# RG-LRU and gates in buffers of their own beside the RWKV, its products in halves of two PSUM banks, and the input projection in five passes

## The chip, the cores and the metric

The kernel runs on one core of one Trainium2 chip. The metric is device time in microseconds of one execution; the time before is the median of three. One further execution was profiled, and its trace gives every duration below. Engines: PE (matrix products), DVE (vector), ACT (scalar), POOL (GpSimd) and SP, whose queue issues the transfers here.

## The reference, cut to what matters

One block of a hybrid encoder, 2048 tokens behind 16 meta tokens, width 1024, float32. Three head groups read the same normed input through one projection; their outputs go through one output projection, then a feed-forward part (FFN) with a convolution.

```python
p = rms_norm(h, norm_mix_pre[l]) @ w_in[l]
pa = p[..., :A_COLS]                     # 512 columns: RG-LRU, xa and ya
pb = p[..., A_COLS:A_COLS + B_COLS]      # q, k, v of 512 columns, 8 forget gates
pc = p[..., A_COLS + B_COLS:]            # 1024 columns: RWKV-7
oa = rg_lru_group(xa, ya, ...)           # conv of 4, two gates, h = a * h + b over time, times gelu(ya)
ob = forgetting_attention_group(...)     # causal softmax(q k + c_i - c_j) v, c = cumsum(log sigmoid(gate))
oc, v_own = rwkv7_group(pc, ...)         # S = S diag(w) - (S kk)(kk a)^T + v k^T over time, o = S r
mixed = jnp.concatenate([oa, ob, oc], axis=-1) @ w_out[l]
h = h + rms_norm(mixed, norm_mix_post[l])
f = causal_dwconv(rms_norm(h, norm_ffn_pre[l]) @ ffn_up[l], ffn_conv[l])
gate, val = jnp.split(f, 2, axis=-1)
f = (jax.nn.gelu(gate, approximate=True) * val) @ ffn_down[l]
h = h + rms_norm(f, norm_ffn_post[l])
```

RG-LRU and RWKV run over time, so their token blocks come one after the other; attention needs the keys and values of all earlier tokens and the sums of the gates.

## The kernel before, in words

The program is written with a tile framework: pools give named tiles with a number of buffers (`bufs`), and a scheduler orders each engine's instructions, by and large as the code is written. Each engine and SP's queue works through its row in order.

- **Input projection.** The tokens come in three parts of 7, 6 and 4 token tiles (784, 768 and 512 tokens), each in two blocks. For a part, `w_in_norm` loads x, norms it on DVE and ACT (L96, `xt` at L108) and transposes it on PE (tile `pst`, L121), with a split into a high and a low half (`xh` L127, `xl` L128). `w_in_part` then goes through units: the gates (tile `psf`), 8 units "c" (RWKV), 4 "a" (RG-LRU), 4 each of k, v and q. Each loads its weights (L143, 512 KB, tile `raw`) and makes three products for one (`mm3`, L150 to L152, tile `psp`). ACT and DVE take the results out of PSUM (`stp`, `sth`, `stl`, `stv`), and SP stores them in DRAM (`scr_p`, `scr_qh`, `scr_kl` and so on).
- **Recurrences.** `Beside(PACE)` advances a generator 1.5 steps for each unit of the projection. `recurrences` runs, for a part, the gates' sums (`gate_block`, L345 to L389), and for three blocks of tokens each `lru_block` (L1228 to L1281), the RWKV block (`R.block`, products in the tiles `eps` and `rps`) and the ending of the block before, one after the other. LRU and gates borrow RWKV's tiles k, r, sq, e and raw. All short products (`eps`) share one PSUM bank, tag "ae", one product at a time. PSUM stands at 5 banks for the projection (`ps_mm`), 1 for "ae", 2 for `rps`.
- **Sums of FFN weights.** `weight_sums` makes sums of blocks of the FFN's weights on POOL (L1436) in one buffer: 22 steps `us` (load L1441, store L1450) and 10 steps `ds` (load L1454, store L1463), each of 2 MB.
- **Attention.** It starts behind the last unit: half 0 is the first half of the queries (from the first K load), in which 8 heads load K, V and Q, PE makes maxima (`mx`) and scores (`sc`), ACT the exponentials (`p`, L558), POOL the masks and sums (`acc`, L588), PE the products with v (`po`), DVE the maxima (`mc`, L492, L495) and the output (`o`). What is left of the recurrences lies in half 0.
- Then follow the other half, the output projection and the FFN.

Of the kernel before, what the change touches and what calls it, by code (L numbers as in the profile page):

```python
# [257 lines left out]
def w_in_part(core, pools, psum, w_in, blocks, scr):  # L258
    yield from w_in_gate(core, pools, psum, w_in, blocks, scr)
    units = [("c", 2056 + P * i) for i in range(8)] + [("a", P * i) for i in range(4)]  # L260
    units += [(s, c + P * i) for s, c in (("k", 1024), ("v", 1536), ("q", 512)) for i in range(4)]
# [77 lines left out]
def gate_block(core, R, f_bias, scr, tl):  # L339
# [10 lines left out]
    x = new("k")  # L350
    nc.sync.dma_start(x, scr["f"][:, t0 : t0 + n])
    a = new("r")
# [7 lines left out]
    call = R.t([NH, 512], "sq")[:, : o + n]  # L360
# [7 lines left out]
    ch, cl = new("k", F32R), new("r", F32R)  # L368
# [304 lines left out]
def columns(core, pool, psum, vecs, name, out=None):  # L673
# [9 lines left out]
    while todo:  # L683
# [6 lines left out]
        if at == P or not todo:  # L690
            ps = psum.tile([P, 512], F32, tag="ae", bufs=1, name=core.n("pscol"))
# [21 lines left out]
def rwkv_consts(core, pool, psum, w):  # L713
# [34 lines left out]
    ps = psum.tile([P, 512], F32, tag="ae", bufs=1, name=core.n("psspr"))  # L748
# [31 lines left out]
    rst = c.tile([P, 8 * CH], F32, name="rst")  # L780
# [6 lines left out]


    u1 = c.tile([P, 256], F32, name="unit1")
    nc.vector.memset(u1[:], 0.0)  # L790
    nc.vector.memset(u1[:, 0:256:17], 1.0)
    u2 = c.tile([P, 128], F32, name="unit2")
    nc.vector.memset(u2[:], 0.0)
    nc.vector.memset(u2[0:64, 0:128:17], 1.0)
    nc.vector.memset(u2[64:128, 8:128:17], 1.0)
    k["unit"] = {1: u1, 2: u2}
# [3 lines left out]
class Rwkv:  # L800
# [23 lines left out]
    def pe(self):  # L824

        return self.epsum.tile([P, 512], F32, tag="ae", name=self.core.n("eps"), bufs=1)

    def raw(self, row, c0, c1):

        raw = self.t([P, 2, 260], "raw", bufs=2)[:, :, : c1 - c0]  # L830
# [13 lines left out]
    def block(self, b):  # L844
# [22 lines left out]
        for p in range(2):  # L867
            cs_ = slice(P * p, P * p + P)
            ps = self.pe()
            nc.tensor.matmul(ps[:, :n], k["up"][0:64, cs_], flat(wa[:])[0:64], start=True, stop=True)  # L870
            nc.scalar.activation(flat(half(sig, p)), ps[:, :n], AF.Tanh, scale=0.5, bias=pcol("w0_h", p))
        nc.gpsimd.tensor_scalar(sig, sig, 0.5, 0.5, op0=ALU.mult, op1=ALU.add)
        for p in range(2):
            cs_ = slice(P * p, P * p + P)
            ps = self.pe()
            nc.tensor.matmul(ps[:, :n], k["up"][64:128, cs_], flat(wa[:])[64:128], start=True, stop=True)
            nc.scalar.activation(flat(half(av, p)), ps[:, :n], AF.Tanh, scale=0.5, bias=pcol("a0_h", p))
# [5 lines left out]
        for p in range(2):  # L883
            nc.tensor.matmul(ps[:4, :n], k["gat"][:, p], flat(half(sq, p)), start=p == 0, stop=p == 1)
        ks2, kinv, ktmp = (self.t([P, 256], s)[:4, :n] for s in ("ia", "ix", "itmp"))
# [3 lines left out]
        nc.vector.tensor_tensor_scan(  # L889
            flat(cs), k["rst"][:, : 2 * n], flat(sig), 0.0, op0=ALU.mult, op1=ALU.add  # L890
        )
# [9 lines left out]
        for p in range(2):  # L901
            ps = self.pe()
            nc.tensor.matmul(ps[:, :n], k["spr"][:, p], kinv, start=True, stop=True)
            stt(flat(half(kt, p)), flat(half(kt, p)), pcol("k_k", p), ps[:, :n], op0=ALU.mult, op1=ALU.mult)
# [15 lines left out]
        for p in range(2):  # L920
            stt(half(kp, p), half(kp, p), pcol("r_k", p), half(r, p), op0=ALU.mult, op1=ALU.mult)
            ps = self.pe()
            nc.tensor.matmul(ps[:, :n], k["bones"][:], flat(half(kp, p)), start=True, stop=True)
            tt(half(bon, p), ps[:, :n].rearrange("p (c t) -> p c t", t=CH), half(rav, p)[:, :, 2], op=ALU.mult)
# [3 lines left out]
    def chunks(self, b, nch, sg, rav, bk, wc, bon):  # L928
# [55 lines left out]
        nc.vector.tensor_copy(ix[:np_, : 16 * jw], k["unit"][parts][:np_, :])  # L984
# [237 lines left out]
def lru_block(core, R, scr, k, b):  # L1222
# [7 lines left out]
    def tl(s):  # L1230
        return R.t([P, 2, 256], s)[:, :, :n]

    raw = R.raw(0, c0 - 3, c0 + n)
    u, r, g = tl("k"), tl("r"), tl("sq")
    e = R.t([P, 2, 2, 256], "e")
    al, y = e[:, 0, :, :n], e[:, 1, :, :n]
    for p in range(2):
# [9 lines left out]
        ps = R.pe()  # L1247
        nc.tensor.matmul(ps[:, :n], k["ga_w"][:, p], up, start=True, stop=True)
        nc.scalar.activation(r[:, p], ps[:, :n], AF.Abs, bias=k["ga_b"][:, pc])
        nc.vector.tensor_scalar(al[:, p], ps[:, :n], k["ga_b"][:, pc], 0.0, op0=ALU.add, op1=ALU.min)  # L1250
        ps = R.pe()
        nc.tensor.matmul(ps[:, :n], k["gx_w"][:, p], up, start=True, stop=True)
        nc.scalar.activation(g[:, p], ps[:, :n], AF.Tanh, scale=0.5, bias=k["rate"][:, 2, pc])
# [4 lines left out]
    yield  # L1258
    for p in range(2):
        pc = slice(p, p + 1)  # L1260
        nc.scalar.activation(al[:, p], r[:, p], AF.Exp, scale=k["rate"][:, 0, pc])
        nc.scalar.activation(r[:, p], r[:, p], AF.Tanh, scale=k["rate"][:, 1, pc])

# [4 lines left out]
    stt(g, g, 0.5, r, op0=ALU.mult, op1=ALU.mult)  # L1268
    for p in range(2):
# [4 lines left out]
    ya = R.raw(256, c0, c0 + n)  # L1274
# [721 lines left out]
```

## Time and profile before

| | us |
|---|---|
| median of 3 runs | 3178.94 (3169.02 to 3179.52) |
| profiled execution, its own time | 3171.78 |
| span of its trace | 3170.1 |
| projection, last product psp | to about 905 |
| K loads of attention's half 0 | from 908 |
| last instruction of the recurrences | about 1231 |
| end of attention's half 0 | about 1240 |
| first product of the output projection | 1290 |
| FFN up | from about 1704 to 2700 |

A window's row gives its bounds and length, the busy time of the engines with the number of instructions, then the granted clock of PE, the DMA share, and GB/s. A row of a wait gives engine, tile and line, what it waited for, the total, the number of waits and the longest. A row of a group ends with minimum, median and maximum in ns, and the first and last start in us. A matmul of plain float32 mostly stands as two records in the trace and as one in the order of instructions.

### The profile page before, as it was taken

The page shows a single profiled execution, that of the slowest core. Times are in us where ns is not written, and L with a number is a line of the kernel's source. Part 1 is how long each engine was busy: PE and PEld are TensorE (multiplying, and loading weights), DVE is VectorE, ACT ScalarE, POOL GpSimd, SP SyncE. Part 2 cuts the span into 40 slices and gives each one's busy share as a digit, 9 for nine tenths or more (in the row PEclk, how much of TensorE's full clock was granted, in tenths as well). Part 3 has the DMA queues.
Part 4 walks back from the last instruction along what each step waited for, and adds up shares of the span by engine and source line. Part 5 has one row for each costly group of instructions (what it writes and reads, how often), then busy time and mean ns, then how long its engine had stood idle before and what let it go on. Part 6 is the DMA issues. An engine that isn't in the chain of part 4 may idle for free. (4 is left out here: it accounts for less than half of the span.)

```text
span 3170.1 us, 53032 instructions
## 1 busy us (share of the span) xinstructions
PE 2974.7 (94%) x18509; PEld 2476.6 (78%) x18509; DVE 2194.2 (69%) x4603; ACT 1444.0 (46%) x2723; POOL 1267.2 (40%) x1439
## 2 busy tenths in 40 slices
PE   6988899999989998999999799999999999999998
PEld 6977788888865554455447699999999999787776
DVE  6247665776677767677756777787778787557777
ACT  4134334344534434444443466666666665424322
POOL 3333343201023344444651234433543334556655
PEclk9989899999987778999999999999999999999999
DMA  6777766543342226444426365555555565535444
GB/s 198 232 225 241 212 196 225 189 132 104 98 124 67 71 64 154 108 109 106 99 59 207 119 181 177 166 170 167 165 167 164 169 187 160 184 103 170 140 160 140
DMA packets 494412, 484.12 MB, mean 153 GB/s; under 512 B 83680, under 2 KB 408618, under 8 KB 488496
## 3 DMA queue, kind: packets, MB, share of 16 engines
q1 hardware_dynamic: 493248, 480.26, 50.8%
q8 instruction: 146, 2.39, 0.3%
q14 instruction: 122, 1.00, 0.1%
q0 software_dynamic: 384, 0.39, 0.0%
q10 hardware_dynamic: 512, 0.07, 0.0%
HBM read 354.66 MB, written 125.87 MB: 152 GB/s over the span
## 5 line engine op out<-in xcount | busy, mean ns | idle before, releaser
L150 PE MATMUL psu<-xo,uw 128*128 128x344 f32 x1848 | 587.8, 323 | 8.2 <-DVE wx L1346 4.8
L151 PE MATMUL psu<-xo,uw 128*128 128x344 f32 x1848 | 593.0, 321 | 1.0 <-DVE xo L1418 1.0
L152 PE MATMUL psu<-xo,uw 128*128 128x344 f32 x1848 | 582.6, 320 | 0.0
L152 PE MATMUL psp<-xh,wl 128*128 128x384 f32 (+2 forms) x1152 | 380.3, 330 | 1.1 <-DVE wl L145 1.0
L150 PE MATMUL psp<-xh,wh 128*128 128x384 f32 (+2 forms) x1152 | 381.2, 331 | 0.0
L151 PE MATMUL psp<-xl,wh 128*128 128x384 f32 (+2 forms) x1152 | 378.2, 328 | 0.0
L150 PEld LDWEIGHTS psu<-xo,uw 128*128 128x128 f32 x1848 | 347.0, 189 | 9.7 <-DVE wx L1346 5.2
L151 PEld LDWEIGHTS psu<-xo,uw 128*128 128x128 f32 x1848 | 348.4, 189 | 1.3 <-DVE xo L1418 1.3
L152 PEld LDWEIGHTS psu<-xo,uw 128*128 128x128 f32 x1848 | 346.8, 189 | 0.0
L1417 ACT ACTIVATE uw<-uq 128x512 fp32r<-128x512 f32 x462 | 286.9, 626 | 98.3 <-PE psu L152 47.8
L1418 DVE TENSOR_TENSOR uw<-uq,uw 128x512 fp32r<-128x512 f32 x330 | 285.5, 869 | 63.6 <-ACT uw L1417 59.2
L558 ACT ACTIVATE p<-sc,bias 128x512 f32<-128x512 f32 (+2 forms) x360 | 203.3, 586 | 254.5 <-PE sc L556 215.9
L588 POOL TENSOR_TENSOR acc<-acc,p 128x512 f32<-128x512 f32 (+3 forms) x208 | 226.9, 1091 | 181.8 <-ACT p L558 152.6
L1418 POOL TENSOR_TENSOR uw<-uq,uw 128x512 fp32r<-128x512 f32 x132 | 180.9, 1370 | 266.6 <-ACT uw L1417 232.5
L1517 DVE SCALAR_TENSOR_TENSOR uy<-psu,ffn_cols,uy 128x342 f32<-128x342 f32 (+1 forms) x396 | 224.0, 568 | 88.2 <-ACT uy L1515 87.1
L1523 POOL TENSOR_TENSOR uy<-uy,uy 128x342 f32<-128x342 f32 (+1 forms) x132 | 136.7, 1036 | 326.1 <-DVE uy L1517 136.5
L492 DVE TENSOR_REDUCE mc<-mx 128x1 f32<-128x400 f32 (+5 forms) x320 | 173.2, 556 | 111.4 <-PE mx L489 110.0
L152 PEld LDWEIGHTS psp<-xh,wl 128*128 128x128 f32 x1152 | 220.0, 191 | 8.2 <-issue 3.7
L151 PEld LDWEIGHTS psp<-xl,wh 128*128 128x128 f32 x1152 | 219.8, 191 | 7.8 <-issue 6.4
L150 PEld LDWEIGHTS psp<-xh,wh 128*128 128x128 f32 x1152 | 220.0, 191 | 6.0 <-issue 3.8
L1436 POOL TENSOR_TENSOR us<-us 128x512 f32<-128x512 f32 x88 | 128.3, 1458 | 221.0 <-DMA us<-in_ffn_up_dram 197.3
L567 PE MATMUL po<-p,v 128*64 128x512 f32 (+3 forms) x720 | 186.3, 555 | 8.4 <-ACT p L558 2.9
(415 smaller groups left out, 6442.1 us busy)
## 6 DMA issues: line engine op xcount, KB each, us to landing
uq<-scr_us SPq DMA_DIRECT2D x264, 256.0 KB
uq<-in_ffn_up_dram SPq DMA_DIRECT2D x198, 256.0 KB
raw<-in_w_in_dram SPq DMA_DIRECT2D x72, 512.0 KB
us<-in_ffn_up_dram SPq DMA_DIRECT2D x44, 512.0 KB
scr_us<-us SPq DMA_DIRECT2D x22, 1024.0 KB
u<-scr_ff SPq DMA_DIRECT2D x88, 256.0 KB
scr_ff<-uy SPq DMA_DIRECT2D x110, 171.0 KB
q<-scr_qh SPq DMA_DIRECT2D x96, 128.0 KB
```

The costliest lines, as they stand in the source:

```text
L150: nc.tensor.matmul(out, ah, bh, start=first, stop=False, skip_group_check=more)
L151: nc.tensor.matmul(out, ah, bl, start=False, stop=False, skip_group_check=more)
L152: nc.tensor.matmul(out, al, bh, start=False, stop=last, skip_group_check=more)
L492: self.reduced = nc.vector.tensor_reduce(mc[:rows, i, ci : ci + 1], ps[:rows, :full], axis=AX.X, op=ALU.max)
L558: last = nc.scalar.activation(p[:rows, :w], ps[:rows, :w], AF.Exp, bias=bias[:rows, j : j + 1])
L567: mm = nc.tensor.matmul(po[64 * i : 64 * i + 64, c0:n], v1[:rows, j], p[:rows, : n - c0], start=jj == 0, stop=jj + i + 2 >= len(kt), tile_ ...
L588: eng.tensor_tensor(a, ps_[0][:rows, c0:n] if jj == 0 else a, p[:rows, : n - c0], op=ALU.add)
L1417: core.nc.scalar.activation(hi, src, AF.Copy)
L1418: (eng or core.nc.vector).tensor_tensor(lo, src, hi, op=ALU.subtract)
L1436: add, sub = (lambda o, x, y, op=op: nc.gpsimd.tensor_tensor(o, x, y, op=op) for op in (ALU.add, ALU.subtract))
L1517: stt(y[:, :n], src[:, i : n + i], cw[:, 44 * i + cc : 44 * i + cc + 1], y[:, :n], op0=ALU.mult, op1=ALU.add)
L1523: core.pooled = nc.gpsimd.tensor_tensor(v[:, :n], g[:, :n], v[:, :n], op=ALU.mult)
```

## The change

- The gates and RG-LRU get tiles of their own (lu, lr, lg, la, lraw). Two operations of RG-LRU go from DVE to POOL. `lru_block` yields at five places, and `recurrences` advances the gates and LRU one step beside each step of the RWKV block, and the ending of the block before likewise.
- The tag "ae" has two banks, `ps_mm` four. `pe2` lays the products of both halves into one bank: two products, then both results are taken out. The scan over a block becomes two of half length; two constant tables go, memsets on POOL replace them.
- The projection goes through five passes: parts 0 and 1 with the columns of the recurrences alone, part 2 with all, then parts 1 and 0 with k, v and q. Parts 0 and 1 are normed and transposed twice (30 token tiles in all for 17). The recurrences of a part join at the unit behind the recurrent columns, `PACE` is 2.5 times the part's share of 768 tokens.
- `weight_sums` works in half tiles (64 steps with four loads and a store), one or two steps per unit from the third pass on, each held behind the SP instruction that stands last in the code at that time (`issue_after`).

PE, transition from the first to the second part. Before: in the tiles, `pst` are the transposes of the new part, `eps` the recurrence's products.

```order
L121 MATMUL pst_2882<-ident,xt_2867 128x128 x4
L121 MATMUL pst_2889<-ident,xt_2867 128x128 x4
L121 MATMUL pst_2911<-ident,xt_2896 128x128 x4
L121 MATMUL pst_2918<-ident,xt_2896 128x128 x4
L870 MATMUL eps_2229<-rwwa_2210,wa_up 128x256
L121 MATMUL pst_2940<-ident,xt_2925 128x128 x4
L121 MATMUL pst_2947<-ident,xt_2925 128x128 x4
L121 MATMUL pst_2969<-ident,xt_2954 128x128 x4
L121 MATMUL pst_2976<-ident,xt_2954 128x128 x4
L870 MATMUL eps_2232<-rwwa_2210,wa_up 128x256
L876 MATMUL eps_2236<-rwwa_2210,wa_up 128x256
```

After, the same transition (the first of four):

```order
L121 MATMUL pst_153_1326<-ident_58,xt_150_1311 128x128 x4
L873 MATMUL eps_189_1525<-rwwa_183_1506,wa_up_1174 128x256
L873 MATMUL eps_190_1530<-rwwa_183_1506,wa_up_1174 128x256 x2
L121 MATMUL pst_154_1333<-ident_58,xt_150_1311 128x128 x4
L121 MATMUL pst_158_1355<-ident_58,xt_155_1340 128x128 x4
L121 MATMUL pst_159_1362<-ident_58,xt_155_1340 128x128 x4
L883 MATMUL eps_192_1539<-rwsq_191_1536,gat_1183 4x256 x2
L121 MATMUL pst_163_1384<-ident_58,xt_160_1369 128x128 x4
```

The products of the recurrences stand in pairs now, and still between the transposes.

PE at the start of attention. Before (`sc` and `mx` are attention's; `rps` and `eps` are the recurrences'; the rows follow the last product of the projection):

```order
L555 MATMUL sc_11063<-q_1503_11001,k_1493_10974 16x16
L489 MATMUL mx_11008<-k_1494_10975,q_1496_10979 16x16
L555 MATMUL sc_11134<-q_1511_11022,k_1493_10974 128x512
L1155 MATMUL rps_8427<-ident,rww_903_6516 128x128 x2
L1159 MATMUL rps_8430<-rwsg_6171,g_up 128x256
L507 MATMUL mx_11015<-ident,sh_11012 1x16
L489 MATMUL mx_11029<-k_1494_10975,q_1501_10989 128x144
L1155 MATMUL rps_8435<-ident,rww_903_6516 128x128 x2
```

After:

```order
L1021 MATMUL rps_9841<-rwxu_9745,rwsc_8604 32x32 x16
L497 MATMUL mx_11743<-k_1536_11710,q_1538_11714 16x16
L563 MATMUL sc_11798<-q_1545_11736,k_1535_11709 16x16
L1021 MATMUL rps_9859<-rwxf_9752,rwxu_9745 32x32 x16
L1061 MATMUL rps_9962<-rww_1128_8605,rwsc_8604 64x64 x8
L515 MATMUL mx_11750<-ident,sh_11747 1x16
L497 MATMUL mx_11764<-k_1536_11710,q_1543_11724 128x144
L563 MATMUL sc_11869<-q_1553_11757,k_1535_11709 128x512
```

Before, the ending of one block (L1155, L1159) stands between attention's products, and RWKV and LRU blocks that begin later follow it; after, the last RWKV block, in its inversion (L1021) and chunks. Of the tile rps 828 of 2164 products stand behind the last projection product before, 301 after; of eps 32 before, none after.

SP at the first K loads of attention. Before:

```order
L453 DMA k_1494_10975<-scr_kh 64x1040
L456 DMA k_1493_10974<-scr_kh 64x1040
L457 DMA k_1493_10974<-scr_kl 64x1040
L454 DMA k_1494_10975<-scr_ch 1x1040
L455 DMA k_1494_10975<-scr_cl 1x1040
L458 DMA v_1495_10976<-scr_v 128x8x64
L459 DMA v_1495_10976<-scr_v 16x64
L476 DMA q_1496_10979<-scr_qh 64x16
```

After (`ds` is the tile of the weight sums):

```order
L1470 DMA ds_9615<-in_ffn_down_dram 128x256 x4
L464 DMA k_1535_11709<-scr_kh 64x1040
L465 DMA k_1535_11709<-scr_kl 64x1040
L466 DMA v_1537_11711<-scr_v 128x8x64
L467 DMA v_1537_11711<-scr_v 16x64
L484 DMA q_1538_11714<-scr_qh 64x16
L485 DMA q_1545_11736<-scr_qh 64x16
L486 DMA q_1545_11736<-scr_qh 64x16
L487 DMA q_1539_11717<-scr_ql 64x16
L1476 DMA scr_ds<-ds_9615 512x1x256
```

Before, the last `ds` load stands 162 rows ahead of the first K load; after, 17 half steps of `ds` stand behind it, between the loads of K, V and Q.

The diff, cut to its core:

```diff
+RECURRENT = [("c", 2056 + P * i) for i in range(8)] + [("a", P * i) for i in range(4)]
+ATTENDED = [(s, c + P * i) for s, c in (("k", 1024), ("v", 1536), ("q", 512)) for i in range(4)]
...
-        return self.epsum.tile([P, 512], F32, tag="ae", name=self.core.n("eps"), bufs=1)
+        return self.epsum.tile([P, 512], F32, tag="ae", name=self.core.n("eps"), bufs=2)
+
+    def pe2(self, n):
+
+        ps = self.pe()
+        return [ps[:, 256 * p : 256 * p + n] for p in range(2)]
...
-        nc.vector.tensor_copy(ix[:np_, : 16 * jw], k["unit"][parts][:np_, :])
+        nc.gpsimd.memset(ix[:np_, : 16 * jw], 0.0)
+        for q in range(parts):
+            nc.gpsimd.memset(ix[q * nblk : (q + 1) * nblk, 8 * q : 16 * jw : 17], 1.0)
...
-    raw = R.raw(0, c0 - 3, c0 + n)
-    u, r, g = tl("k"), tl("r"), tl("sq")
+        return R.t([P, 2, 256], "l" + s)[:, :, :n]
+
+    raw = R.raw(0, c0 - 3, c0 + n, "lraw", 1)
+    u, r, g, al = tl("u"), tl("r"), tl("g"), tl("a")
...
-    nc.vector.tensor_scalar(y, y, 0.044715, 1.0, op0=ALU.mult, op1=ALU.add)
-    tt(y, y, ya, op=ALU.mult)
+    nc.gpsimd.tensor_scalar(y, y, 0.044715, 1.0, op0=ALU.mult, op1=ALU.add)
+    nc.gpsimd.tensor_tensor(y, y, ya, op=ALU.mult)
...
-    for k in range(DOWN_PAIRS):
-        t = pool.tile([P, 4, 512], F32, tag="us", name=core.n("ds"))
-        nc.sync.dma_start(
-            t[:].rearrange("p (i h) c -> p i (h c)", h=2),
-            w_down[2 * P * k : 2 * P * (k + 1), :].rearrange("(i p) c -> p i c", p=P),
-        )
+    for k, half in ((k, half) for k in range(DOWN_PAIRS) for half in range(2)):
+        t = pool.tile([P, 4, 256], F32, tag="us", name=core.n("ds"))
+        for i in range(4):
+            r0, c0 = P * (2 * k + i // 2), 512 * (i % 2) + 256 * half
+            nc.sync.dma_start(t[:, i], w_down[r0 : r0 + P, c0 : c0 + 256])
...
-PACE = 1.5
+PACE = 2.5
+
+
+PASSES = (0, True, False), (1, True, False), (2, True, True), (1, False, True), (0, False, True)
...
-    def advance(self):
-        self.due += self.pace if self.gens else 0.0
+    def advance(self, share):
+        self.due += self.pace * share if self.gens else 0.0
...
-    for blk in blocks:
-        gate_block(core, R, f_bias, scr, blk[2])
-        yield
-    for b in ((0, 1, 2), (3, 4, 5), (6, 7, 8))[part]:
-        yield from lru_block(core, R, scr, lk, b)
+    beside = others()
+    for b in RW_BLOCKS[part]:
         gen = R.block(b)
         while next(gen) != R.SOLVED:
+            next(beside, None)
             yield
+        for _ in R.ending:
+            next(beside, None)
+            yield
+        R.ending = gen
+    yield from beside
...
-            ps_mm = pool(p1a, "ps_mm", 5, space=PSUM)
+            ps_mm = pool(p1a, "ps_mm", 4, space=PSUM)
...
-            for part in range(3):
+            for at_, (part, recurrent, attended) in enumerate(PASSES):
...
+                    if due:
+                        beside.add(recurrences(core, R, lk, a["fox_f_bias"], scr, due[1], due[0]))
+                        due = None
+                    if recurrent and i == READY:
+                        due = part, blocks
+                    beside.advance(share)
+                    for _ in range(1 + i % 2 if at_ > 1 else 0):
+                        with tc.issue_after(transfer()):
+                            next(sums, None)
```

`others()` gives the gate blocks and then the steps of the LRU blocks; `transfer()` returns SP's last instruction so far.

More of the change, by code (lines that the diff above doesn't have):

```diff
@@ L888, in block @@
         yield
-        nc.vector.tensor_tensor_scan(
-            flat(cs), k["rst"][:, : 2 * n], flat(sig), 0.0, op0=ALU.mult, op1=ALU.add
-        )
+        for p in range(2):
+            nc.vector.tensor_tensor_scan(
+                flat(half(cs, p)), k["rst"][:, :n], flat(half(sig, p)), 0.0, op0=ALU.mult, op1=ALU.add
+            )
         tt(sig, cs, sig, op=ALU.subtract)
@@ L900, in block @@
         tt(kp[:], kt[:], kp[:], op=ALU.mult)
[L901 to L904, printed above, removed]
+        pss = self.pe2(n)
+        for p, ps in enumerate(pss):
+            nc.tensor.matmul(ps, k["spr"][:, p], kinv, start=True, stop=True)
+        for p, ps in enumerate(pss):
+            stt(flat(half(kt, p)), flat(half(kt, p)), pcol("k_k", p), ps, op0=ALU.mult, op1=ALU.mult)
         kk = kt[:]
@@ L1807, in hybrid_block_kernel, with transfer @@
             following = w_in_norm(core, pools, ps_mm, x, meta, g_pre, 0)
-            for part in range(3):
+            due, beside = None, Beside(PACE)
+            def transfer():
+                return next(i for i in reversed(nc.cur_bb.bb.instructions) if i.engine == mybir.EngineType.SP)
+            for at_, (part, recurrent, attended) in enumerate(PASSES):
                 blocks = following
-                if part == 0:
+                if at_ == 0:
                     zeros = pools["st"].tile([P, PAD], F32, tag="sth", name="zeros")
@@ L1838, in hybrid_block_kernel @@
-                for i, _ in enumerate(units, READY + 1 if part == 0 else 1):
-                    if i == READY + 1:
-                        beside.add(recurrences(core, R, lk, a["fox_f_bias"], scr, blocks, part))
-                    beside.advance()
-                    if part and i % 3:
-                        next(sums, None)
-                run(sums) if part == 2 else None
-                if part < 2:
-                    following = w_in_norm(core, pools, ps_mm, x, meta, g_pre, part + 1)
+                share = sum(n for _, n, *_ in blocks) / 768
@@ L1847, in hybrid_block_kernel @@
+                if at_ + 1 < len(PASSES):
+                    following = w_in_norm(core, pools, ps_mm, x, meta, g_pre, PASSES[at_ + 1][0])
+            run(sums)
         beside.finish()
```

172 lines of the change are left out of this document (88 added, 84 removed).

## The prediction

> **What bounds the kernel now.** I read the page first, then windows by stage, the waits of PE, and the groups of single tiles. In the page's slices (79 us each) PE is the row near 9 almost everywhere; the slices that stand out are 12 to 16, where PEclk falls.
>
> ```profile
> PE 2974.7 (94%) x18509; PEld 2476.6 (78%) x18509; DVE 2194.2 (69%) x4603; ACT 1444.0 (46%) x2723; POOL 1267.2 (40%) x1439
> PE   6988899999989998999999799999999999999998
> DVE  6247665776677767677756777787778787557777
> PEclk9989899999987778999999999999999999999999
> ```
>
> The change ends with attention's half 0 (about 1240 us); from there on both kernels issue the same work. So only the time up to 1240 is in dispute. The windows (PE, PEld, DVE, ACT, POOL busy, then the granted clock and the DMA share):
>
> ```profile
> 0.00:300.00 300.00, 256.18 (x1363) 243.29 (x1364) 151.51 (x356) 98.47 (x170) 103.30 (x100) 0.97 0.73 223
> 300.00:330.00 30.00, 14.33 (x62) 10.41 (x61) 26.07 (x55) 19.26 (x37) 16.61 (x16) 0.66 0.86 240
> 330.00:640.00 310.00, 294.02 (x2364) 267.31 (x2363) 197.45 (x416) 114.82 (x202) 106.17 (x111) 0.97 0.64 203
> 640.00:905.00 265.00, 257.54 (x2757) 231.94 (x2755) 182.32 (x406) 121.82 (x227) 27.07 (x48) 1.00 0.38 108
> 905.00:1240.00 335.00, 296.25 (x2309) 180.86 (x2309) 243.66 (x830) 126.00 (x300) 120.02 (x223) 0.77 0.37 90
> ```
>
> The projection lasts to 905 us, and PE is busy for 256.18 + 14.33 + 294.02 + 257.54 = 822 of it: PE bounds it, with 83 us of gaps, 16 of them in the 30 us of the first change of token parts. Half 0 lasts 335 us; no engine is full, PE runs at a clock of 0.77, and DVE is busy for 73%. There DVE carries two jobs, attention's maxima and what is left of the recurrences; this window is where the change can gain.
>
> PE's gaps up to 905 us (line waited for, total, times, longest):
>
> ```profile
> PE pst L121 <- DVE xt L108: 19.2, 4, 10.8
> PE eps L870 <- ACT rwe L871: 9.0, 3, 8.3
> PE eps L1252 <- DVE rwe L1250: 8.7, 3, 7.5
> PE eps L386 <- DVE ccol L378: 7.8, 2, 7.0
> PE eps L870 <- ACT rwsq L1253: 3.5, 2, 3.0
> ```
>
> Two kinds: waits for the one bank "ae" (29.0 us in these four eps rows) and the transposes that wait for the norm on DVE (19.2).
>
> **The change, part by part.**
>
> *Recurrences move ahead of attention.* Share of the recurrences: the tile rps on PE (first two rows), eps (last two), before and behind 905 us.
>
> ```profile
> 0.00:905.00 905.00, 139.42 (x2560) 117.26 (x2560) 65.76 (x137) 33.80 (x67) 0.97 0.60 183
> 905.00:1240.00 335.00, 111.34 (x1602) 91.89 (x1602) 40.96 (x96) 21.28 (x44) 0.77 0.37 90
> 0.00:905.00 905.00, 69.31 (x219) 31.18 (x219) 22.33 (x58) 26.01 (x56) 0.97 0.60 183
> 905.00:1240.00 335.00, 21.27 (x62) 10.81 (x62) 6.62 (x18) 6.38 (x16) 0.77 0.37 90
> ```
>
> In the order of before 828 of 2164 rps products stand behind the last projection product (38%, the same share as 1602 of 4162 records); now 301 (14%). So 24.4% of 4162, or 1014 records, move forward: at 139.42 / 2560 = 54.5 ns they add 55 us to PE. All eps products move: 62 records at 0.316 us, 20 us. Of DVE's recurrence instructions 343 stand behind attention's first before, 93 now: 73% go.
>
> *Five passes for three.* The weight loads (first row below, 512 KB each) and their products stay as many; what is added is 13 token tiles (30 for 17) that are normed and transposed again. Their cost, by the tiles pst (PE, PEld, DVE, ACT; second row) and xt (the same):
>
> ```profile
> raw<-in_w_in_dram SPq DMA_DIRECT2D x72, 512.0 KB
> ...
> 0.00:905.00 905.00, 26.92 (x136) 21.87 (x136) 21.37 (x34) 18.29 (x34) 0.97 0.60 183
> 0.00:905.00 905.00, 26.92 (x136) 21.87 (x136) 23.53 (x17) 19.46 (x34) 0.97 0.60 183
> ```
>
> Per tile 26.92 / 17 = 1.58 us of PE and (21.37 + 23.53) / 17 = 2.6 us of DVE, beside small ones. Thirteen: PE +21, DVE +34. The x loads (13 more, 512 KB) lie beside a DMA share of 0.6. What is exposed is the idle PE at a change of parts. The first one in slices of 10 us:
>
> ```profile
> 300.00:310.00 10.00, 4.88 (x30) 3.76 (x29) 7.08 (x13) 5.59 (x13) 6.89 (x8) 0.80 0.67 193
> 310.00:320.00 10.00, 2.64 (x12) 2.23 (x11) 9.02 (x28) 8.69 (x13) 2.67 (x4) 0.67 1.02 296
> 320.00:330.00 10.00, 6.81 (x21) 4.42 (x22) 9.97 (x16) 4.98 (x11) 7.05 (x5) 0.50 0.90 231
> ```
>
> PE loses 16 us, DVE is full. The first transition of after (no recurrence has gone far by then) is like this one. Three follow; the order puts many recurrence products just ahead of each, as before's second transition had, inside the window 640 to 905 with 7 us of gaps in all. So the two additional ones cost between 0 and 2 x 16 = 32 us; I take 16, since DVE has more to do per us now. On the clock, the Trainium skill ("TensorE: Matmul & The Clock Gate", section "HAM oscillation — how this bites in real kernels") says that a PE gap of more than about 3.4 us drops the clock to half. The 0.50 of the third slice agrees. By that rule a transition also slows the products behind it, an estimated 5 us for 10 us at half clock, so twice 5 us would come on top, and the sum would end at 3168 us.
>
> *Two banks, products in pairs.* A pair now needs one bank and waits once; the next pair has the other bank. That removes between none and 29.0 us of the eps waits shown. I take 27: the longest in the first three eps rows, 8.3, 7.5 and 7.0 us, are waits of a product for an operand late behind the single bank in PE's order, or for the bank itself, and the gate and LRU blocks are now spread over the steps of RWKV. The price, one ps_mm bank less of five, stands against psp evacuations that no quoted wait names: 0, up to a few us if ACT and DVE fall behind.
>
> So the projection ends at 905 + 55 + 20 + 21 - 27 + 16 = 990 us. Bounds: 972 (29 us of waits gone, no transition) and 1033 (no waits gone, 32 us of transitions).
>
> *LRU and gate in own tiles; small edits.* Two DVE operations per LRU block go to POOL, 9 blocks, hidden by POOL's 40%; the scan in halves adds one instruction per block, the POOL memsets replace a DVE copy. Their sum is under 10 us on DVE and either sign: 0. If POOL were late, the next step of the LRU chain (L1279) would wait, not PE, whose rows of LRU come earlier.
>
> *Half 0.* DVE's work there is attention's by the tiles mx, o, sh and acc (third, first, third and third busy column):
>
> ```profile
> 905.00:1240.00 335.00, 79.17 (x207) 31.20 (x207) 68.74 (x188) 15.02 (x47) 0.77 0.37 90
> 905.00:1240.00 335.00, 31.45 (x47) 4.88 (x15) 0.77 0.37 90
> 905.00:1240.00 335.00, 6.87 (x25) 2.02 (x25) 11.01 (x50) 0.77 0.37 90
> 905.00:1240.00 335.00, 21.24 (x44) 1.90 (x44) 7.19 (x22) 9.43 (x22) 66.88 (x82) 0.77 0.37 90
> ```
>
> 68.74 + 31.45 + 11.01 + 7.19 = 118, about 138 with the bias, reciprocals and memsets; the other 105 of 243.66 are recurrences. With 73% of these gone 167 remain; at the same busy share of 0.727 half 0 takes 229 us. Bounds: at a share of 0.80, 209; if only the 64% of the rps products count, 176 / 0.727 = 242.
>
> *Weight sums in half tiles, bound to SP's place.* Before they ran at 26 to 594 us; now 17 of the 20 ds half steps stand behind the first K load on SP, and between attention's selects on POOL. One buffer: load, four POOL operations, store, then the next load.
>
> ```profile
> L1441 SPq DMA_DIRECT2D us<-in_ffn_up_dram x44: 367/416/1417, 25.8 to 418.0; - x44
> L1436 POOL TENSOR_TENSOR ds<-ds x40: 1262/1289/2162, 437.7 to 593.7; 128x512 f32<-128x512 f32 x40
> L1454 SPq DMA_DIRECT2D ds<-in_ffn_down_dram x10: 373/383/1580, 432.6 to 583.0; - x10
> POOL us L1436 <- DMA us<-in_ffn_up_dram: 197.3, 18, 18.2
> ```
>
> A full step took (583.0 - 432.6) / 9 = 16.7 us, 5.2 of it POOL (4 x 1.289). A half step is between 8.4 (all of it halves) and 14.3 us (only POOL halves, the rest 11.5 stays). I take the middle, 11.3: 17 x 11.3 = 192 us, under the 229 of half 0, so hidden; at 14.3 it is 243 and sets the end. The cover is half 0 itself; when it is gone, POOL waits in order for a load with the selects behind it, and PE's po waits for those. SP issues 320 transfers for these sums, 86 before: 234 x 0.38 = 89 us more of issuing over 1200 us, beside waits; 0, with q and K loads queued behind it.
>
> Sum: half 0 ends at 990 + 229 = 1219 for 1240, a gain of 21 us. The profiled execution took 3171.78 us (span 3170.1), 7 under the median of 3178.94; against the median 21 less is **3158 us**.
>
> **Rivals.**
>
> *More gain.* For it: 640 to 905 shows that PE with much recurrence work beside it loses only 7 of 265 us, and half 0 has the low clock of 0.77 that denser work may lift. Against it: DVE is near full wherever a norm runs. With the projection at 972 and half 0 at 209: 1181, 59 less, 3120 us.
>
> *The work only moves.* PE's own work up to 1240 is the same plus 21 us. Its gaps were 83 + 39 = 122 us; if gaps stay, only the clock gains, 1014 x (69.5 - 54.5) ns = 15 us. Then +6: 3185 us. For it: PE is the bound in the windows up to 905; against: the 39 us and the clock stand where DVE has two jobs, and one leaves.
>
> *Slower: the sums set half 0.* Steps gain nothing from halving (16.7 us, since flow and waiting are per transfer, and the loads now wait in SP's order behind K and q loads that wait for buffers): 17 x 16.7 = 284 us, the end at 990 + 284 = 1274, +34: 3213 us. It decides from 229 / 17 = 13.5 us a step on. For it: the 197.3 us POOL waited for such loads (18 times, 11 each); against: those fell in a DMA share of 0.73, half 0 has 0.37 with half the bytes. On transfers that do not shrink, the Trainium skill ("DMA: Bandwidth & Descriptors", section "Anatomy of one DMA — SWDGE (gpsimd) path") gives about 2 us that are fixed for each; by it a half step is an estimated 2 x 2 + (11.5 - 4) / 2 + 2.6 = 10.4 us, which no row here shows and which would leave half 0 at 229 us.
>
> **How the numbers follow.** A measurement of this kernel can tell about 0.5% (16 us). Chances: forecast 0.42, own range 3130 to 3188; more gain 0.18; only moved 0.18; sums set half 0 0.22. The forecast lies near the edge of 3163, so it gives 0.24 to faster and 0.17 to same; more gain is faster; only moved gives 0.02, 0.11 and 0.05; the sums' case is slower but for 0.01. Faster 0.45, same 0.28, slower 0.27. The range goes from the gain case with a bit of clock (3105) to the sums' case with 10 us of transitions (3222).
>
> **What would show it.** Right: the last psp at about 990; after the first K load few rps rows; half 0 about 229 us with the clock over 0.85; eps waits gone from PE's list; sums' steps of 11 to 12 us. Wrong: PE waits on po or sc released by POOL selects and POOL by DMA ds (the sums); four windows like 310 to 320 (the transitions); DVE over 90% busy around 600 to 990, with PE waiting for DVE tiles; a last rps row still past half 0's end.

## The result, and the profile after

The changed kernel takes 3271.07 us (median of 4 runs, 3267.1 to 3282.27) for 3178.01 before: 93 us slower, ratio 1.0305 (95% interval 1.0272 to 1.0337). The forecast was 3158 with a range of 3105 to 3222. The profiled execution of the changed kernel has a span of 3265.4 us. Its page, first the totals and then the slices (82 us each):

```profile
PE 3019.4 (92%) x18613; PEld 2517.2 (77%) x18613; DVE 2217.2 (68%) x4736; ACT 1474.3 (45%) x2775; POOL 1330.7 (41%) x1611
PE   7889999899898877899999889999999999899998
POOL 1011243233333565443573224533443333556655
PEclk9989999999798677899999999999999999999999
```

The slices in which PE falls behind and its clock is low lie at 1060 to 1310 us now, which is attention's half 0. POOL, nearly idle at 0 to 320 us, is busy there: the last of the weight sums went there (all of them run from 364 to 1256 us now, 26 to 595 before). Windows up to the last psp, and from there to the first product of the output projection; two rows of before, then two of after (PE, PEld, DVE, ACT, POOL, clock, DMA share):

```profile
0.00:902.00 902.00, 820.73 (x6535) 752.15 (x6536) 554.45 (x1227) 353.78 (x633) 250.91 (x270) 0.97 0.60 183
902.00:1290.00 388.00, 340.73 (x2479) 201.69 (x2477) 286.21 (x912) 154.01 (x347) 152.22 (x254) 0.79 0.41 99
```

```profile
0.00:1037.00 1037.00, 931.07 (x7717) 848.71 (x7718) 658.59 (x1620) 426.42 (x790) 279.75 (x411) 0.93 0.52 152
1037.00:1378.00 341.00, 272.90 (x1396) 143.16 (x1394) 205.23 (x647) 109.27 (x239) 185.82 (x285) 0.74 0.59 154
```

The work moved as the order said: 1083 PE records and 81 us of DVE left half 0. But the projection became 135 us longer and half 0 only 47 us shorter; from the output projection on, both kernels need nearly the same (1880 and 1887 us). In half 0 no engine is full after the change: PE is busy for 80%, at a clock of 0.74, and DVE for 60%.

### The profile page after: what moved, and what is told of

Same layout as the page of the kernel before. It is cut to its first block, busy times and chain, and to the rows that moved or that the text cites. A ratio compares the mean times of both kernels' runs of the same rounds, so it can differ in the third digit from the quotient of the medians.

```text
span 3265.4 us, 54095 instructions
## 1 busy us (share of the span) xinstructions
PE 3019.4 (92%) x18613; PEld 2517.2 (77%) x18613; DVE 2217.2 (68%) x4736; ACT 1474.3 (45%) x2775; POOL 1330.7 (41%) x1611
## 5 line engine op out<-in xcount | busy, mean ns | idle before, releaser
L1451 POOL TENSOR_TENSOR us<-us 128x256 f32<-128x256 f32 x176 | 150.1, 853 | 244.3 <-DMA us<-in_ffn_up_dram 187.2
```

Source lines behind the costliest of these rows:

```text
L1451: add, sub = (lambda o, x, y, op=op: nc.gpsimd.tensor_tensor(o, x, y, op=op) for op in (ALU.add, ALU.subtract))
```

## The experiments

Each run was compared with the kernel before on the same chip; "stages" gives the last psp and the first pswo (first product of the output projection) of its profile: 902 and 1290 before, 1037 and 1378 after. Half 0 is counted from one to the other here, 388 us before. The prediction ended it at 1240 and had 335 us, so its forecast of 229 corresponds to about 282 here.

**Passes and sums undone.** `e1_sums_free` drops `with tc.issue_after(transfer())`.

> The changed kernel, but the half-tile weight sums are not held behind SP's transfers any more: the scheduler may start them early, as before the change; no sum stands behind the first K load. Theory A (the two additional passes cost the time: 13 more token tiles, more transitions): projection still ends at 1030 to 1045 us, half 0 as long as now, total 3265 to 3280. Theory B (the sums between attention's selects on POOL and its K and q loads on SP slow half 0): half 0 (last psp to first pswo, 341 us now) falls to about 290, total about 3220. If early sums crowd the projection's DMA, the last psp goes 10 to 20 us later.

3284.23 us, ratio 1.0337 (1.0313 to 1.036); stages 1095 and 1393. Half 0 falls to 298 us, as theory B said, but the projection grows by 58 for it, not by 10 to 20, and the total does not fall. The half sums cost time wherever they lie.

```diff
-PASSES = (0, True, False), (1, True, False), (2, True, True), (1, False, True), (0, False, True)
+PASSES = (0, True, True), (1, True, True), (2, True, True)
...
-                    for _ in range(1 + i % 2 if at_ > 1 else 0):
+                    for _ in range(1 + i % 2 if at_ > 0 else 0):
```

With three passes the sums begin in the second pass, in place of the third.

> The changed kernel with three passes as before (each part with all columns); own buffers, two banks, pairs, pace and held sums stay. Theory A: the last psp goes from 1037 back to 920 to 950 us; more recurrence products (654 for 301) lie in half 0, which takes up to 370 us instead of 341; total 3170 to 3200. Theory B: sums still lie in half 0 (18 half steps), so less than 30 us of the 93 come back: 3240 or more.

3253.27 us, ratio 1.024 (1.0215 to 1.0264); stages 952 and 1369. The projection is 85 us shorter, half 0 is 76 longer: the two additional passes cost 18 us by the medians and are not what costs most. Theory A falls.

> Three passes and sums not held: only the own buffers, the two banks with pairs, the pace and the half tiles of the change are left. Theory A alone: as with three passes and held sums, 3170 to 3200. Both theories: 40 to 50 us less than that, 3130 to 3150, below the kernel before. If own buffers, pairs and banks are worth nothing: 3178.

3288.99 us, ratio 1.0346 (1.0322 to 1.037); stages 1008 and 1411. Both theories are wrong: with the passes and the hold undone, the kernel is no faster than the changed one (the intervals overlap).

`e4_one_bank` is the changed kernel with `bufs=1` for the tag "ae" and five banks in `ps_mm`.

> The changed kernel with one bank for the short products (pairs stay) and five for the projection. The prediction gave two banks 27 us: then about 3298. If the pairs alone bring that, or the waits were hidden: 3265 to 3278. If the fifth bank of the projection was worth more (DVE and ACT take psp results out late): below 3262.

3245.33 us, ratio 1.0217 (1.0199 to 1.0236); stages 989 and 1370. The second bank (with the projection's fifth given up for it), to which the prediction gave a gain of 27 us, costs 26.

**Parts of the change on the kernel before, and the sums taken out.** `e5_before_half_sums` puts the new `weight_sums` into the kernel before (called more often, for its 64 steps); `e6_before_pairs` puts `pe2` with two banks and four for `ps_mm` there.

> The kernel before with the half-tile weight sums alone (64 steps of four loads and a store, free to start early). Theory C (the halved sums crowd SP's queue and the projection, whatever holds them): the last psp moves from 902 to 930 us or later, total 3205 to 3260. If the halves are harmless by themselves: 3178 within 16 us, and the loss sits in buffers, banks or pace.

3231.67 us, ratio 1.0166 (1.0151 to 1.0181); stages 970 and 1345. The halves alone cost 54 us: theory C.

> The kernel before with the two banks, the products in pairs and four banks for the projection alone. The prediction gave them 27 us of gain: 3150. Theory D (one bank less for the projection costs more than the second bank brings, as the one-bank run of the changed kernel suggests): 3190 to 3210. Neither: 3178 within 16.

3256.59 us, ratio 1.025 (1.023 to 1.0271); stages 917 and 1361. Of the 71 us by which the output projection starts later, 56 arise in half 0. Of this kernel: the last eps product, the last psp and attention's first mx (last two columns of a row: first and last start).

```profile
L925 PE MATMUL eps<-rwsq,bones x36: 379/400/795, 240.1 to 1035.8; 128*128 128x256 f32 x32, 128*128 128x64 f32 x4
...
L150 PE MATMUL psp<-xh,wh x1152: 274/337/668, 49.4 to 917.2; 128*128 128x384 f32 x95, 128*128 128x256 f32 x64, 128*128 128x400 f32 x33
...
L489 PE MATMUL mx<-k,q x360: 183/394/795, 1059.8 to 1702.2; 128*128 128x512 f32 x77, 128*128 128x400 f32 x53, 128*128 128x128 f32 x14, 128*128 128x256 f32 x14
```

Attention starts at 1060, 143 us behind the last psp and 24 behind the last eps. By the code its PSUM pool follows `ps_mm`, of which one bank less is left; it has five tiles of a bank each (two `sc`, two `mx`, one `po`), and the fifth is a bank of the short products. With five banks (`e13_before_pairs_one_bank`) the same rows read:

```profile
L925 PE MATMUL eps<-rwsq,bones x36: 275/379/634, 252.2 to 1090.5; 128*128 128x256 f32 x32, 128*128 128x64 f32 x4
...
L150 PE MATMUL psp<-xh,wh x1152: 274/337/882, 43.3 to 919.0; 128*128 128x384 f32 x95, 128*128 128x256 f32 x64, 128*128 128x400 f32 x33
...
L489 PE MATMUL mx<-k,q x360: 172/393/811, 934.9 to 1621.6; 128*128 128x512 f32 x77, 128*128 128x400 f32 x57, 128*128 128x256 f32 x14, 128*128 128x128 f32 x13
```

Attention starts 16 us behind the last psp, with eps products still to come until 1090, and the whole is 86 us faster than e6 (by the ratios).

`e7_after_no_sums` and `e8_before_no_sums` never call `weight_sums`.

> The changed kernel without weight sums (the FFN reads plain weights in their place, so its result is not the block's). Theory C: the last psp falls from 1037 to 990 or earlier and half 0 from 341 to below 300 us, total below 3190. Theory A (passes): the last psp stays over 1020, total over 3220.

> The kernel before without weight sums (the FFN reads plain weights in their place, so its result is not the block's). The price of the sums where they lay before: if they were nearly hidden, the last psp stays within 10 us of 902 and the total within 16 of 3178; if they cost there too, 20 us or more less. The difference to the changed kernel without sums is the price of everything else in the change.

e7: 3156.95 us (7 runs, 3147.27 to 3172.05; the profiled one is the slowest), e8: 3126.27 (2 runs). Windows of e7 and e8, as above:

```profile
0.00:978.00 978.00, 913.39 (x7718) 837.80 (x7719) 638.13 (x1623) 426.32 (x790) 120.77 (x223) 0.95 0.39 111
978.00:1284.00 306.00, 260.69 (x1407) 138.85 (x1405) 197.11 (x650) 110.86 (x243) 136.15 (x219) 0.80 0.48 113
```

```profile
0.00:848.00 848.00, 807.15 (x6539) 742.94 (x6539) 511.39 (x1228) 355.44 (x633) 68.76 (x142) 0.97 0.40 116
848.00:1235.00 387.00, 335.18 (x2472) 199.41 (x2471) 284.42 (x910) 154.53 (x344) 150.94 (x254) 0.81 0.42 99
```

So the sums cost 114 us in the changed kernel (by the medians) and 50 before: 64 of the 93. Everything else in the change costs 31 by the medians, 47 by the profiled executions (3170.3 and 3123.7). There the projection is 130 us longer, half 0 is 81 shorter. By the profiled executions the sums take 54 us of the projection and 1 of half 0 before (848 and 387 without them), 59 and 35 after: the steps that left the projection did not relieve it.

**Where the sums cost, and which bank.** `e9_three_one_bank` is e2 and e4 together; `e10` is e5 with `pool(p1a, "us", 2)`; e11 and e12 issue the sums' transfers with `nc.gpsimd.dma_start`.

> The changed kernel with three passes and one bank for the short products (five for the projection): own buffers, pairs, pace and held half sums stay. Theory F (with four projection banks attention's PSUM tiles must wait for a bank of the short products, so that half 0 starts only behind the last eps product): here attention's first product follows the last psp within 25 us although eps products come later, and the total falls by 25 us or more below the 3253 of three passes with two banks. If three passes cost what they cost for another reason: 3245 to 3260.

3237.44 us, ratio 1.0183 (1.0166 to 1.02); stages 933 and 1359. Attention's first mx starts at 952, 19 behind the last psp, as theory F said; the total falls by 16 only, not by 25.

> The kernel before with half-tile sums in two buffers (the same space as one whole tile). Theory G (one buffer makes SP wait in its order for POOL and then for the store's landing, 64 times for 32; this blocks the loads and stores behind): the load waits for a store two steps back, so most of the 56 us that halves cost come back, total 3195 or less. Theory H (the transfers themselves, more and smaller, cost the time): 3225 to 3240.

3230.49 us, ratio 1.0171 (1.0141 to 1.0202); stages 934 and 1343. The projection gets 36 us of the halves' cost back, as theory G has it, and the total nothing. The last store of the RWKV chain, the loads of the output projection's weights and the first pswo tell why; before, e5 and e10 in turn (the last two numbers ahead of the semicolon are the first and last start):

```profile
L1169 SPq DMA_DIRECT2D scr_mix<-rwxu x1: 377/377/377, 1230.7 to 1230.7; - x1
...
L143 SPq DMA_DIRECT2D raw<-in_w_out_dram x8: 327/372/579, 1232.9 to 1267.9; - x8
...
L150 PE MATMUL pswo<-woh,mh x272: 387/389/796, 1290.5 to 1791.6; 128*128 128x512 f32 x128, 128*2 128x512 f32 x8
```

```profile
L1169 SPq DMA_DIRECT2D scr_mix<-rwxu x1: 382/382/382, 1281.1 to 1281.1; - x1
...
L143 SPq DMA_DIRECT2D raw<-in_w_out_dram x8: 327/371/529, 1286.0 to 1324.5; - x8
...
L150 PE MATMUL pswo<-woh,mh x272: 387/389/792, 1345.2 to 1844.1; 128*128 128x512 f32 x128, 128*2 128x512 f32 x8
```

```profile
L1169 SPq DMA_DIRECT2D scr_mix<-rwxu x1: 382/382/382, 1284.9 to 1284.9; - x1
...
L143 SPq DMA_DIRECT2D raw<-in_w_out_dram x8: 328/348/530, 1287.1 to 1324.5; - x8
...
L150 PE MATMUL pswo<-woh,mh x272: 387/389/796, 1342.7 to 1848.4; 128*128 128x512 f32 x128, 128*2 128x512 f32 x8
```

The output projection starts 60, 64 and 58 us behind that store, whatever the projection does (e10's last psp is 36 us earlier than e5's). By the code the pool of its weights follows the pools of the recurrences; its loads begin 2 to 5 us behind the chain's last store. So in these kernels the serial chain of nine RWKV blocks ends the stage. In the changed kernel it does not:

```profile
L1176 SPq DMA_DIRECT2D scr_mix<-rwxu x1: 382/382/382, 1149.8 to 1149.8; - x1
...
L143 SPq DMA_DIRECT2D raw<-in_w_out_dram x8: 328/368/531, 1318.6 to 1355.3; - x8
...
L150 PE MATMUL pswo<-woh,mh x272: 387/389/793, 1378.1 to 1880.5; 128*128 128x512 f32 x128, 128*2 128x512 f32 x8
```

Here 228 us of attention follow the chain's last store, and the weights are loaded 169 us behind it. (In e6, where attention starts late, the last store is at 1159 and the first pswo at 1361.)

> The changed kernel with the sums' loads and stores issued by POOL's queue instead of SP's. Theory G: SP no longer waits for sums, and the last psp falls from 1037 to 1000 or earlier; total 3225 or less, unless POOL's own issuing holds up its work for RWKV and attention. Theory H: 3260 to 3285. POOL issuing too dear: over 3290.

3229.5 us, ratio 1.0155 (1.0133 to 1.0178); stages 1033 and 1352. 42 us less, but not where theory G put it: the last psp moves by 4 us, half 0 by 22, since the sums were done by 1004 us. More than the queue changes here: the sums' loads begin at 14 us, for 364 in the changed kernel, so `issue_after` did not hold them back in POOL's queue. Nearer is e1, whose sums start early too (25 us) and go by SP: against it the last psp is 61 us earlier and the total 55 less, which speaks for theory G, though its mark of 1000 us is missed.

> The kernel before with the whole-tile sums' transfers issued by POOL's queue instead of SP's. Without any sums it took 3126. Theory G: a good part of these 50 us are SP's waits, total 3140 to 3160. Theory H: 3170 to 3185. POOL's issuing too dear: over 3190.

3239.99 us, ratio 1.0197 (1.0182 to 1.0212); stages 965 and 1357. POOL's queue is too dear here, and theory G is no general answer. Of POOL's waits in the projection the first is before its own loads:

```profile
POOL us L1441 <- issue: 109.0, 22, 6.2
```

**The chain and the parts of the halves.**

> The kernel before with the products in pairs, but one bank for them and five for the projection as before. Theory I (in kernels like the one before, the output projection starts about 95 us behind the last store of the RWKV chain, so what shortens the chain of nine blocks shortens the time): pairs with two banks shortened the chain from first to last scan from 819 to 786 us; if the pairs do this without the second bank, the last store falls from 1196 to 1150 to 1170 and the total to 3135 to 3160. If the gain came from the second bank: 3165 to 3190.

3170.06 us, ratio 0.998 (0.9964 to 0.9997); stages 919 and 1286, last store 1228. The projection is 17 us longer and the stage ends 4 us earlier, 58 behind that store: the chain again. (The last store of the kernel before stands at 1231, 60 us ahead of the output projection; the 1196 and 95 of theory I are those of the block before the last.) Pairs alone do not shorten it: 833 us from first to last scan, 819 before and 786 in e6, so there it was the second bank. A second trace (`e15`, 3169.43 us) has stages 917 and 1282.

> The same kernel as the pairs with one bank once more, for a second trace: the last psp, the last store of the chain and the start of the output projection within 10 us of the first.

`e14_before_held_sums` wraps the kernel before's `next(sums, None)` into `tc.issue_after(transfer())`; e16 does so in e13.

> The kernel before with its whole-tile sums held behind SP's transfers (two of three units of the second and third part), so that they no longer stand at 33 to 594 us but where POOL was busy for 27 of 265 us. Theory I with sums that delay the chain's POOL work where they run: the early blocks speed up as without sums (scans at 204, 292, 372), the late ones slow down; total between 3126 and 3178 if POOL's idle late time takes them, 3178 to 3210 if each sum delays the chain wherever it stands.

> Pairs in one bank and held whole-tile sums on the kernel before: if both help, the sum of their two differences, at best 3100; if the chain's POOL waits are only moved, as the better of the two alone.

e14: 3190.48 us, ratio 1.0047 (1.0032 to 1.0062); e16: 3190.28, 1.0049 (1.0033 to 1.0066). In e14 the early scans stand at 204, 291 and 370 us (230, 324, 414 before), as without sums, and the last at 1066 (1049): what the early blocks win, the late ones lose. e16 is as slow as e14, not as fast as the better of the two.

> The kernel before with whole tiles and 32 steps, but each step's transfers cut as in the halves (eight loads and two stores). The halved sums cost 56 us. If the transfers carry it (more to issue on SP, smaller packets): 3215 to 3240. If the 64 rounds through one buffer carry it: 3178 within 16 us.

> The kernel before with whole tiles and whole transfers, but eight POOL operations of 128x256 per step for four of 128x512. The 256 operations of the halves took 220 us on POOL, the 128 whole ones 183. If POOL's instructions carry the cost of the halves (37 us more, in front of the RWKV chain's POOL work): 3200 to 3240; if not: 3178 within 16 us.

e17: 3218.14 us, ratio 1.012 (1.0102 to 1.0138). e18: 3186.8, ratio 1.0031 (1.0017 to 1.0044). The cut transfers alone carry 38 to 40 of the halves' 54 us, as expected if they carry the cost; the short operations 9 to 10, within the 16 us that stood for nothing. What is left for the 64 rounds is within the intervals. The projection of e17 ends at 955, 52 us later than before. DMA packets of before, e17 and e18:

```profile
DMA packets 494412, 484.12 MB, mean 153 GB/s; under 512 B 83680, under 2 KB 408618, under 8 KB 488496
```

```profile
DMA packets 534512, 484.16 MB, mean 150 GB/s; under 512 B 87424, under 2 KB 455370, under 8 KB 532688
```

```profile
DMA packets 494413, 484.13 MB, mean 152 GB/s; under 512 B 83680, under 2 KB 408618, under 8 KB 488496
```

The same bytes go in 40,100 packets more, and in 320 issues on SP for 86. Which of the two it is, no run tells.

## Why the prediction was wrong, point by point

By the ratios the change (1.0305, 97 us) comes apart like this, as a ladder whose rungs are runs:

| step | ratio to before | added |
|---|---|---|
| halved sums alone (e5) | 1.0166 | 53 us |
| + own buffers, pairs, pace, sums held; three passes, one bank (e9) | 1.0183 | 5, not told from nothing |
| + five passes (e4) | 1.0217 | 11, intervals touch |
| + second bank for the short products, four for the projection (after) | 1.0305 | 28 |

In another order the shares differ: the second bank costs 18 with three passes (e9 to e2), the five passes 21 with two banks (e2 to after). No run has the changed kernel with whole-tile sums; the 53 us were measured on the kernel before.

- **Halved sums at nothing.** This is the step that failed first, in two ways. It was priced as a race of 17 steps of 11.3 us against half 0, with half 0 as cover. (The upper bound of a step should read 11.5 + 2.6 = 14.1, not 14.3, which decides nothing.) The steps took 12.9 us (loads from 1006.3 to 1251.5 us over 19 steps), more than the 11.3 and than the 10.4 of the prediction's other estimate:

```profile
L1470 SPq DMA_DIRECT2D ds<-in_ffn_down_dram x80: 333/428/1382, 1006.3 to 1251.5; - x80
L1451 POOL TENSOR_TENSOR ds<-ds x80: 715/726/1287, 1009.1 to 1255.8; 128x256 f32<-128x256 f32 x80
```

  The last POOL operation on them begins 122 us ahead of the first pswo, so the slow rival (16.7 us a step, the sums set the end) did not happen either. Yet half 0 is 341 us with them and 306 without (e7), 298 and 319 where they run earlier (e1, e11). POOL waits for their loads in half 0, with attention's work behind in its row, and PE waits more for loads of Q; the first two rows are of the changed kernel, the last is all that e7 has on these loads:

```profile
POOL ds L1451 <- DMA ds<-in_ffn_down_dram: 52.0, 24, 7.1
...
PE mx L497 <- DMA q<-scr_qh: 6.7, 4, 3.0
...
PE sc L563 <- DMA q<-scr_qh: 2.8, 2, 2.4
```

  PE's own waits for POOL's sums are 0.5 us there, those for Q's loads from `scr_qh` 10.9 (2.8 in e7), and PE is busy 12 us longer for nearly the same products, at a clock of 0.74 for 0.80. Which of these carries the 35 us stays open. So what hid beside the stage in length still cost time. The other part was overlooked: the cost outside half 0. SP's 234 additional issues were set at 0; the cut transfers alone cost 38 to 40 us in the kernel before (e17). In the changed kernel the sums take 59 us of the projection, 54 before, although 17 of the 64 steps had left it.

- **Two banks, 27 us of gain.** The four eps rows of before held 29.0 us. Three of their releasers (L871, L1250, L1253; 21.2 us) are readings of the bank. The fourth (L378, 7.8 us) makes the operand `ccol` of the product that waits (L386), and no second bank takes such a wait away. Nor does a row give the 27: the three longest waits named for it add up to 22.8. After the change the longest eps rows are

```profile
PE eps L904 <- DVE rwkn L77: 7.3, 2, 4.9
PE eps L384 <- DVE rwk L906: 5.5, 2, 2.9
PE eps L1256 <- DVE rwlu L1249: 4.4, 2, 3.5
PE eps L873 <- ACT rwwa L862: 2.8, 2, 2.1
```

  20 us in these four; only L906 reads a bank, the other three (14.5 us) make an operand. Waits of the bank went, others took the place of about half. And the fifth bank of the projection was not free: in the kernel before, its lack holds attention back (e6 against e13, 86 us). In the changed kernel attention does not wait for it (the last eps stands at 963, ahead of the last psp), and the second bank still costs 26: the projection is 48 us longer than e4's, half 0 is 40 shorter. The windows of e4, and of the tile rps with two banks (after), then with one (e4), show what these are:

```profile
0.00:989.00 989.00, 886.25 (x7321) 814.02 (x7322) 636.90 (x1550) 420.30 (x779) 247.95 (x373) 0.95 0.52 152
989.00:1370.00 381.00, 301.51 (x1806) 169.27 (x1805) 227.24 (x723) 116.19 (x255) 208.38 (x326) 0.73 0.58 157
...
0.00:1037.00 1037.00, 209.87 (x3572) 177.49 (x3572) 91.22 (x191) 47.29 (x94) 0.93 0.52 152
...
0.00:989.00 989.00, 181.62 (x3184) 153.56 (x3184) 81.54 (x170) 43.44 (x86) 0.95 0.52 152
```

  With the second bank 388 more records of rps come ahead of the last psp, and PE is busy there for 931 us in place of 886: of the 48 us, 45 are PE's work. The bank let the recurrences get further, into the stage that PE fills; the work moved. The profiled executions differ by 14 us (3265.4 and 3250.9), the medians by 26. Over both stages PE takes 16 us more for the same products (1204 for 1188), and why that is stays open.

- **Projection at 990.** With sums it grew by 135 us (902 to 1037), without sums on both sides by 130 (848 to 978); forecast were 85. Without sums PE's own work grew by 913.4 - 807.2 = 106 us for 96. This term held, with some luck in its parts: 1012 records of rps moved, as forecast (1014), but they added 69 us and not 55, 68 ns each, near the 69.5 that such records cost where they had stood; eps added 10 for 20, and the same psp took 11 more. The gaps grew by (978 - 913.4) - (848 - 807.2) = 24 us, where 16 - 27 = -11 stood. The four transitions of the changed kernel:

```profile
148.00:178.00 30.00, 13.47 (x68) 9.81 (x67) 28.86 (x77) 16.05 (x34) 0.62 (x1) 0.63 0.51 146
343.00:373.00 30.00, 29.25 (x275) 25.57 (x275) 28.01 (x63) 19.85 (x39) 8.16 (x10) 1.00 0.67 177
629.00:659.00 30.00, 22.50 (x238) 19.80 (x237) 25.47 (x72) 13.91 (x25) 1.04 (x2) 0.77 0.57 161
832.00:862.00 30.00, 21.40 (x290) 18.27 (x289) 20.90 (x70) 11.53 (x28) 14.14 (x29) 0.67 0.57 183
```

  lose 17, 1, 8 and 9 us of PE, 33 unrounded, of which the first is like before's 16. So 17 were added for the 16 forecast (12 without the sums, by windows of 30 us in e7); the clock fell to 0.63 to 0.77 in three of them. What failed is the 27 us of the banks: in their place stand 24 - 12 = 12 us of further gaps.

- **Half 0 in 229 us.** The order's 73% held: DVE lost 284.4 - 197.1 = 87 us there without sums (forecast 77). The scaling failed: at a fixed busy share of DVE 77 us of work were to bring 106. Half 0 gave 387 - 306 = 81, about one for one: DVE's idle time was 103 us before and 109 after (136 with the sums), its share fell from 0.73 to 0.64. PE lost 74 us there too, and its share stayed (0.87 and 0.85); in the prediction's own window it is 296.25 of 335, fuller than DVE's. The step took DVE for what sets the stage's length, and no run shows that. What the runs show is that the RWKV chain ended the stage before (e5, e10, e13) and that attention ends it after. The clock, forecast above 0.85, was 0.74 (0.80 without sums).

- **The rivals.** "The work only moves" (3185) named the mechanism best: e9 to e4 shows 56 us more of projection against 45 less of half 0, e4 to after 48 against 40. It had no term for the sums. Of the signs of failure, POOL's waits for ds are there, PE's waits behind them hardly. And 47 of the 113 us between forecast and result lie in the projection (1037 for 990), for which no sign named the sums' transfers.

## What to carry to other kernels

Ask what ends a stage before you scale its length with one engine's work. Here work moved out of half 0 gave back about its own length, not its share of the stage (87 us of DVE, 74 of PE, for 81); moved into a stage in which PE was busy for 91%, it cost its whole length and the gaps around it. Cutting a background transfer into pieces is not free because it is in the background: count its issues and packets, and where they stand in the queue that carries the foreground's loads and stores. Before a PSUM bank goes from one pool to another, look at which pool takes over those banks in the next stage.

## What the runs showed of the hardware that was not expected

- The same 484 MB in 8% more packets (534512 for 494412), with 234 more issues on SP, cost 38 to 40 us of 3178, in a kernel whose transfers take about half of the DMA engines' time (50.8% by the page of before).
- POOL's sums at half the length take 0.73 us for 1.29 (medians of `ds`), and beside the projection 0.85 on average for 1.46 (`us`: 150.1 us in 176, 128.3 us in 88), so halving saved 42 to 44%, less than half.
- 36 us less of projection brought nothing (e10), and 17 us more cost nothing (e13), where a serial chain beside it ended the stage.
